# Sparse-head scores two units ahead, and three differential query projections moved up, in a one-core hybrid attention layer

## The chip, the cores and the metric

The kernel runs on one core of a Trainium2 chip. The metric is the device time of one execution in microseconds (us). TensorE is written PE, its weight loads PEld, VectorE DVE, ScalarE ACT, GpSimd POOL, and SyncE, which issues all DMAs here, SP.

## What is computed

One decoder layer over 1024 tokens of width 1024, batch 1, float32:

```python
h   = x @ w_in                                   # all queries, keys, values and gates
o_diff = diff_attention(dq, dk, dv, ...)         # 4 heads, two softmaxes each: p1 - lam * p2, then RMS norm
o_nsa  = nsa_attention(nq, ...)                  # 8 heads: compressed, selected and window branches, gated
mix = concat([o_diff, o_nsa]) @ w_out
x   = layer_norm(alpha * x + mix)
ffn = (silu(x @ w_gate) * (x @ w_up)) @ w_down   # d_ff = 2816
out = layer_norm(alpha * x + ffn)
```

With 16 selection blocks and top 16, the selected branch sees every causal key, so the kernel computes it as plain causal attention.

## The kernel before

All products of the projections and of the feed-forward part are done three times with float32 operands split in a high and a low half (`mm3`, lines 118 to 120). The keys and queries of attention carry both halves stacked in one 128-row operand, so a score block is two matmuls (lines 313 and 314). In the first 100 us x is loaded and the shared keys and values are made. From there to about 600 us attention runs, then the output projection, and from about 625 us the feed-forward part, whose matmuls stand in a fixed order.

Attention is a list of **units**. A unit of the sparse heads (`nsa_units`) is one pair of heads, one block of 128 queries and one kind, selected or window; eight blocks and two kinds make 16 units for each of four pairs p. A unit of a differential head (`diff_units`) is one head h and one block i. Each unit has two halves:

- the **front**: scores of both heads (or both softmax branches) into a PSUM bank `psS` (two of them in rotation), the addition of the position bias with a running minimum on DVE (line 320), which reads `psS` and writes a score tile `t`; exponentials on ACT (line 334); reciprocals on DVE and scaling on POOL;
- the **back**: transposes of the probabilities into `psT` (line 353 for the sparse heads, 343 for the differential ones), their copies to `pt` on ACT and DVE, and the products with the values into the one bank `psO` (lines 406, 414, 416, and 470).

There are six `t` tiles. A unit wider than 512 keys takes two of them, a narrower one takes one.

Beside the units stand **fillers**, projections that later units need: `qf` and `qdf` for one half (512 tokens) of the queries of a sparse pair or a differential head, `kf` and `kdf` for keys, `dvf` for values of a pair of differential heads. A filler of 512 tokens is 24 matmuls of 512 columns into a bank `psM` (two in rotation). A query half is evacuated by ACT (line 178) and DVE (line 179) and then spread by three DMAs on SP (line 163), of which the third overwrites what the first two read. Query halves live in two pairs of tiles in rotation, so a half can be evacuated only when the scores of the half two before it are done.

`phases` lists, phase by phase, the units, the fillers, and as its last number `look`: how many units may be pending, that is have their front issued and their back not. After each front, backs are issued until no more than `look` are pending. Fillers are handed out in list order in proportion to the backs that are done. Written order gives each instruction a priority (backs 60 lower, fillers 2000 lower than they stand); a scheduler then lays down one fixed order for each engine from priorities, dependences and free buffers. The engines keep that order at run time.

Of the kernel before, what the change touches and what calls it, by code (L numbers as in the profile page):

```python
# [39 lines left out]
def layer_kernel(ctx: ExitStack, tc: tile.TileContext, xT, x, w_t, w_vg, w_dv, lam_in, subln,  # L40
# [24 lines left out]
    def slot(n, dt=F32R, wide=False):  # L65

        w = 1024 + NC if n in (0, 6) else 1024
        t = slots.tile([P, w], dt, tag=f"slot{n}", name=f"slot{n}", bufs=1)
        return t if wide or w == 1024 else t[:, :1024]
# [35 lines left out]
    def w_tiles():  # L105
        lo = w_tile()
        return w_tile(), lo
# [38 lines left out]
    with ExitStack() as ctx_a:  # L146
# [363 lines left out]
        def k_fill(n, where, out, halves=(0, 1)):  # L510
            def steps():
                if 0 in halves:
                    out.extend([slot(m) for m in where])
                    out.append(load_split(w_t[n], *w_tiles(), l_eng="pool", pieces=2))
                for hf in halves:
                    yield from proj_steps(out[2], hf, evac_k(out))
            return steps, 5.2 * len(halves)
# [4 lines left out]
        def q_fill(n, hf, qt, tiles=w_tiles):  # L522

            def steps():
                if hf == 0:
                    qt.append(load_split(w_t[n], *tiles(), l_eng="pool", pieces=2))
                w = qt[0]

                def done(_, ps):
                    q = [q_tile() for _ in range(2)]  # L530
                    evac_q(q, qscale[:, n - 4:n - 3], ps)
                    qt.append(q)
                yield from proj_steps(w, hf, done)
            return steps, 5.2
# [3 lines left out]
        def dv_fill(pair, where, out, blocks, tiles):  # L538
            def steps():
                if pair not in dv_parts:  # L540
                    dv_parts[pair] = [(*load_split(w_dv[pair, :, kk, :], *tiles(kk), l_eng="pool", pieces=2), 4 * kk, 4)
                                      for kk in range(2)]
                parts = dv_parts[pair]
                for i in blocks:
                    if i % 4 == 0:
                        out.append(slot(where[i // 4], F32))
                    ps = ps_m()
                    yield from proj_rows(parts, 256, i, ps)
                    nc.scalar.copy(out[i // 4][:, (i % 4) * 256:(i % 4 + 1) * 256], ps[:, :256])
            return steps, 2.61 * len(blocks)  # L550
# [4 lines left out]
        def wo_copy(nh):  # L555
            def steps():
                for kp in range(KT // 2):
                    nc.sync.dma_start(wo_d[nh, kp], w_out[nh, kp])
                    yield 0.0
            return steps, 0.0  # L560
# [170 lines left out]
        def nsa(p):  # L731
            return lambda: nsa_units(p, qn[p], [KC[p // 2], K[p // 2][1]], [V[0][p // 2], V[1][p // 2]])
# [3 lines left out]
        def diff(h, first=0, last=NB):  # L736
            def f():
                if h not in made:
                    made[h] = diff_units(h, qd[h], kd[h], vd[h // 2])
                return made[h][first:last]  # L740
            return f

        def qf(p, hf):
            return q_fill(4 + p, hf, qn[p])

        def kf(hf):
            return k_fill(3, (), K[1], (hf,))

        def qdf(h, hf, tiles=w_tiles):
            return q_fill(8 + 2 * h, hf, qd[h], tiles)  # L750

        def kdf(h, hf):
            return k_fill(9 + 2 * h, ((0, 1), (2, 4))[h % 2], kd[h], (hf,))

        def dvf(pair, blocks):
            tiles = [lambda kk: w_tiles(), lambda kk: [slot(n) for n in ((10, 11), (3, 5))[kk]]][pair]
            return dv_fill(pair, ((8, 9), (6, 7))[pair], vd[pair], blocks, tiles)
# [7 lines left out]
        def held_fill():  # L765
# [8 lines left out]


        phases = [
            (nsa(0), [qf(0, 1), kf(0), qf(1, 0), kf(1)], 1, 0, 1),
            (nsa(1), [qf(1, 1), dvf(0, range(8)), wo_copy(0), qf(2, 0)], 1, 0, 1),
            (nsa(2), [qf(2, 1), kdf(0, 0), wo_copy(1), qf(3, 0), kdf(0, 1)], 1, 0, 1),
            (nsa(3), [qf(3, 1), kdf(1, 0), qdf(0, 0), kdf(1, 1)], 1, 0, 1),  # L780
            (diff(0), [qdf(0, 1), dvf(1, range(4)), qdf(1, 0)], 1, 0, 1),
            (diff(1), [qdf(1, 1), kdf(2, 0), kdf(2, 1), qdf(2, 0)], 1, 0, 1),
            (diff(2, 0, 4), [kdf(3, 0), kdf(3, 1), qdf(3, 0)], 0, 0, 2),
            (diff(3, 0, 4), [qdf(2, 1), dvf(1, range(4, 8))], 0, 0, 2),
            (diff(2, 4), [wo_fill(0), qdf(3, 1), wo_fill(1), held_fill(), out_fill(0, False), out_fill(1, False)], 0, 0, 2),
# [432 lines left out]
```

## Time and profile before

| | |
|---|---|
| median of 3 runs | 1329.98 us (1327.45 to 1330.0) |
| profiled execution | 1330.6 us, of which the span from the first to the last instruction is 1328.9 us |
| busy share of the span | PE 98%, PEld 83%, DVE 69%, ACT 49%, POOL 35% |
| mean granted TensorE clock | 0.997 |

The profiled execution is one of the kernel's ordinary executions; its own time is 0.6 us above the median. Busy time is the union of an engine's instructions. A matmul's record also covers the time in which its last columns drain, so two matmuls can start up to some 0.17 us later than they could have without any idle time showing between them.

### The profile page before, as it was taken

The numbers are of one execution on the slowest core, as the hardware profiler recorded it, in microseconds if no ns is written. First come the engines' busy times: TensorE is split into PE (matmuls) and PEld (weight loads), VectorE is DVE, ScalarE is ACT, GpSimd is POOL, SyncE is SP. The second block draws the span as 40 slices with busy tenths as digits, with TensorE's granted clock in tenths as the row PEclk, the third lists the DMA queues.
The fourth block names the chain that finished last, engine by engine and source line by source line (L and its number), as shares of the span: only waits on it lengthen the run. The fifth ranks groups of instructions, "written<-read, shape, count | busy, mean of one in ns | idle before, by whom it ended". The sixth has DMA issues, their size and how long they took to land.

```text
span 1328.9 us, 20438 instructions
## 1 busy us (share of the span) xinstructions
PE 1301.0 (98%) x6922; PEld 1106.2 (83%) x6922; DVE 914.9 (69%) x1949; ACT 649.1 (49%) x1398; POOL 469.7 (35%) x504
## 2 busy tenths in 40 slices
PE   9999999999999999999999999999999999999997
PEld 7898998888889878788887888788888888888886
DVE  5536658678798466684688758777777768555588
ACT  5336678676787455653345332332333326533330
POOL 4414354354445336553532222222312232000072
PEclk9999999999999999999999999999999999999999
DMA  9412022130211325533213656655455549768651
GB/s 356 137 26 63 7 59 50 31 80 19 62 24 45 72 60 156 174 102 113 103 72 96 220 191 222 204 169 190 158 191 188 190 147 350 270 202 285 191 171 66
DMA packets 86842, 183.13 MB, mean 138 GB/s; under 512 B 10577, under 2 KB 19153, under 8 KB 86609
## 3 DMA queue, kind: packets, MB, share of 16 engines
q1 hardware_dynamic: 86736, 181.82, 42.4%
q8 instruction: 55, 0.90, 0.3%
q14 instruction: 51, 0.41, 0.1%
HBM read 116.18 MB, written 57.15 MB: 130 GB/s over the span
## 4 chain that ended last, share of the span: by engine, by line
PE 86%; DVE 6%; DMA 3%; ACT 2%; issue 2%; POOL 0%; POOLq 0%; DVEq 0%; SPq 0%; ACTq 0%
PE psM L118 10%; PE psM L120 10%; PE psM L119 10%; PE psS L120 5%; PE psS L119 5%; PE psS L118 5%; PE psT L118 5%; PE psT L120 5%; PE psT L119 5%; PE psT L353 4%; PE psS L313 3%; PE psS L314 3%; PE psO L470 2%; PE psO L416 2%; PE psO L414 2%
## 5 line engine op out<-in xcount | busy, mean ns | idle before, releaser
L334 ACT ACTIVATE t<-t,m 128x128 f32<-128x128 f32 (+7 forms) x192 | 144.0, 750 | 67.9 <-DVE m L320 64.4
L399 POOL TENSOR_SCALAR t<-t,r,gates 128x640 f32<-128x640 f32 (+7 forms) x128 | 99.6, 784 | 188.7 <-DVE r L393 103.3
L313 PE MATMUL psS<-slot,q 128*128 128x320 f32 (+10 forms) x304 | 113.7, 377 | 8.9 <-DVE m L320 5.8
L118 PE MATMUL psM<-big,w 128*128 128x512 f32 x304 | 121.9, 401 | 0.3
L119 PE MATMUL psM<-big,w 128*128 128x512 f32 x304 | 120.1, 395 | 0.7 <-POOL big L85 0.7
L120 PE MATMUL psM<-big,w 128*128 128x512 f32 x304 | 119.8, 394 | 0.0
L976 POOL TENSOR_TENSOR half<-half,half 128x512 f32<-128x512 f32 x22 | 33.1, 1506 | 200.3 <-ACT half L975 200.3
L85 DVE TENSOR_TENSOR pt<-psT,pt 128x512 fp32r<-128x512 f32 (+1 forms) x152 | 91.2, 613 | 12.3 <-ACT pt L83 11.8
L314 PE MATMUL psS<-slot,q 128*128 128x320 f32 (+10 forms) x304 | 99.3, 329 | 0.0
L83 ACT CAST pt<-psT 128x512 fp32r<-128x512 f32 (+1 forms) x152 | 77.0, 526 | 31.5 <-PE psT L353 23.0
L83 ACT CAST big<-slot 128x1024 fp32r<-128x1024 f32 (+1 forms) x54 | 54.1, 1017 | 74.5 <-DVE slot L968 60.8
L353 PE MATMUL psT<-ident,t 128*128 128x128 f32 x528 | 84.0, 273 | 1.4 <-DVE pt L85 0.9
L85 DVE TENSOR_TENSOR op<-op 128x1024 fp32r<-128x1024 f32 x44 | 60.5, 1382 | 35.5 <-ACT op L83 34.9
L85 DVE TENSOR_TENSOR big<-slot,big 128x1024 fp32r<-128x1024 f32 (+1 forms) x54 | 63.5, 1182 | 29.7 <-ACT big L83 29.7
L313 PEld LDWEIGHTS psS<-slot,q 128*128 128x128 f32 x304 | 57.4, 189 | 24.2 <-DVE m L320 14.1
L83 ACT CAST op<-op 128x1024 fp32r<-128x1024 f32 x44 | 45.8, 1051 | 59.3 <-DMA op<-t_d 52.1
L320 DVE CUSTOM_DVE_ANT_0 t<-psS,dsel 128x384 f32<-128x384 f32 (+9 forms) x128 | 62.5, 493 | 16.5 <-PE psS L314 15.5
L980 POOL TENSOR_TENSOR half<-half,half 128x512 f32<-128x512 f32 x22 | 36.5, 1658 | 105.3 <-DVE half L979 97.8
L416 PE MATMUL psO<-pt,slot 128*128 128x256 f32 x264 | 72.8, 298 | 0.2
L414 PE MATMUL psO<-pt,slot 128*128 128x256 f32 x264 | 71.0, 288 | 0.1
L83 ACT CAST big<-big 128x1024 fp32r<-128x1024 f32 (+1 forms) x49 | 44.3, 913 | 48.8 <-DMA big<-t_d 39.0
L353 PEld LDWEIGHTS psT<-ident,t 128*128 128x128 f32 x528 | 61.7, 140 | 7.4 <-issue 3.2
(368 smaller groups left out, 3961.1 us busy)
## 6 DMA issues: line engine op xcount, KB each, us to landing
a_d<-slot SPq DMA_DIRECT2D x77, 256.0 KB, 3.0
t_d<-slot SPq DMA_DIRECT2D x77, 256.0 KB, 2.2
q<-q SPq DMA_DIRECT2D x48, 256.0 KB, 2.9
slot<-in_w_up_dram SPq DMA_DIRECT2D x22, 512.0 KB, 3.8
slot<-in_w_down_dram SPq DMA_DIRECT2D x22, 512.0 KB, 3.8
op<-a_d SPq DMA_DIRECT2D x44, 256.0 KB, 3.6
op<-t_d SPq DMA_DIRECT2D x44, 256.0 KB, 4.1
big<-a_d SPq DMA_DIRECT2D x33, 256.0 KB, 3.0
```

Of the source, the lines that this page charges most:

```text
L83: nc.scalar.copy(hi, src)
L85: eng.tensor_sub(lo, src, hi.bitcast(F32))
L118: nc.tensor.matmul(acc, lhsT=ah, rhs=bh, start=first, stop=False, skip_group_check=more)
L119: nc.tensor.matmul(acc, lhsT=ah, rhs=bl, start=False, stop=False, skip_group_check=more)
L120: nc.tensor.matmul(acc, lhsT=al, rhs=bh, start=False, stop=last, skip_group_check=more)
L313: nc.tensor.matmul(ps[:, :c + part], lhsT=q[0], rhs=k[:, ks], start=True, stop=False)
L314: nc.tensor.matmul(ps[:, :c + part], lhsT=q[1], rhs=k[:, ks], start=False, stop=True)
L334: nc.scalar.activation(t[:, :width], t[:, :width], AF.Exp, bias=m, scale=-1.0, accum_out=r)
L353: nc.tensor.transpose(tp[:rows, n * P:(n + 1) * P], s, ident)
L399: nc.gpsimd.tensor_scalar(t, t, r[:, c:c + 1], gates[:, i, gc:gc + 1], op0=ALU.mult, op1=ALU.mult)
L414: nc.tensor.matmul(po[:, :256], lhsT=v, rhs=pt[:, 0, n * 256:(n + 1) * 256], start=False, stop=False)
L416: nc.tensor.matmul(po[:, :256], lhsT=v, rhs=pt[:, 1, n * 256:(n + 1) * 256], start=False, stop=last)
```

## The change

`look` of the four sparse phases goes from 1 to 2, and in the phases of differential heads 0 and 1 a query projection moves ahead of other fillers. Nothing else is edited; every instruction is the same and only the order differs.

```diff
-            (nsa(0), [qf(0, 1), kf(0), qf(1, 0), kf(1)], 1, 0, 1),
-            (nsa(1), [qf(1, 1), dvf(0, range(8)), wo_copy(0), qf(2, 0)], 1, 0, 1),
-            (nsa(2), [qf(2, 1), kdf(0, 0), wo_copy(1), qf(3, 0), kdf(0, 1)], 1, 0, 1),
-            (nsa(3), [qf(3, 1), kdf(1, 0), qdf(0, 0), kdf(1, 1)], 1, 0, 1),
-            (diff(0), [qdf(0, 1), dvf(1, range(4)), qdf(1, 0)], 1, 0, 1),
-            (diff(1), [qdf(1, 1), kdf(2, 0), kdf(2, 1), qdf(2, 0)], 1, 0, 1),
+            (nsa(0), [qf(0, 1), kf(0), qf(1, 0), kf(1)], 1, 0, 2),
+            (nsa(1), [qf(1, 1), dvf(0, range(8)), wo_copy(0), qf(2, 0)], 1, 0, 2),
+            (nsa(2), [qf(2, 1), kdf(0, 0), wo_copy(1), qf(3, 0), kdf(0, 1)], 1, 0, 2),
+            (nsa(3), [qf(3, 1), kdf(1, 0), qdf(0, 0), kdf(1, 1)], 1, 0, 2),
+            (diff(0), [qdf(0, 1), qdf(1, 0), dvf(1, range(4))], 1, 0, 1),
+            (diff(1), [qdf(1, 1), kdf(2, 0), qdf(2, 0), kdf(2, 1)], 1, 0, 1),
             (diff(2, 0, 4), [kdf(3, 0), kdf(3, 1), qdf(3, 0)], 0, 0, 2),
             (diff(3, 0, 4), [qdf(2, 1), dvf(1, range(4, 8))], 0, 0, 2),
```

The first place is on PE, where differential head 1 passes from its block 6 (scores of 448 columns) to its block 7 (512 columns). `psS` takes scores, `psT` transposes, `psO` products with values, `psM` fillers. Before:

```order
L313 MATMUL psS<-slot_4550,q 128x448
L314 MATMUL psS<-slot_4550,q 128x448
L313 MATMUL psS<-slot_4550,q 128x448
L314 MATMUL psS<-slot_4550,q 128x448
L313 MATMUL psS<-slot_4549,q 128x512
L314 MATMUL psS<-slot_4549,q 128x512
L313 MATMUL psS<-slot_4549,q 128x512
L314 MATMUL psS<-slot_4549,q 128x512
L313 MATMUL psS<-slot_4550,q 128x512
L314 MATMUL psS<-slot_4550,q 128x512
L488 MATMUL psT<-ident,od 128x128 x4
```

The same four pairs of 512 columns in the changed kernel:

```order
L120 MATMUL psM<-big,w 128x512
L470 MATMUL psO<-slot_2216,pt 128x128 x4
L470 MATMUL psO<-slot_2558,pt 128x128
L313 MATMUL psS<-slot_4565,q 128x512
L488 MATMUL psT<-ident,od 128x128 x4
L314 MATMUL psS<-slot_4565,q 128x512
L313 MATMUL psS<-slot_4565,q 128x512
L314 MATMUL psS<-slot_4565,q 128x512
L343 MATMUL psT<-ident,t 128x128 x6
L313 MATMUL psS<-slot_4566,q 128x512
L314 MATMUL psS<-slot_4566,q 128x512
L343 MATMUL psT<-ident,t 128x128 x4
```

Five pairs that stood back to back are taken apart: fillers and products with values now stand between block 6 and block 7, and transposes between the pairs of block 7.

The second place is on SP, where the queries of differential head 3 (first half) are spread by their three DMAs (`q<-q`), beside loads of the output weights (`wo_d`) and of two rows of x (`in_x_dram`). Before:

```order
L101 DMA big<-wo_d 128x512 x8
L163 DMA q<-q 64x1024 x2
L574 DMA slot_7128<-in_x_dram 128x1024
L574 DMA slot_7239<-in_x_dram 128x1024
L163 DMA q<-q 64x1024
```

In the changed kernel:

```order
L101 DMA big<-wo_d 128x512 x8
L163 DMA q<-q 64x1024 x3
L574 DMA slot_7128<-in_x_dram 128x1024
L574 DMA slot_7239<-in_x_dram 128x1024
```

The third of the moves no longer stands behind the two loads of x.

The third place is on PE, in sparse pair 2, where the selected unit of block 7 (wide scores cut in pieces of 480 and 320 columns) meets the window unit. Before:

```order
L353 MATMUL psT<-ident,t 128x128 x4
L313 MATMUL psS<-slot_547,q 128x480
L314 MATMUL psS<-slot_547,q 128x480
L313 MATMUL psS<-slot_547,q 128x480
L314 MATMUL psS<-slot_547,q 128x480
L313 MATMUL psS<-slot_547,q 128x480
L314 MATMUL psS<-slot_547,q 128x480
L353 MATMUL psT<-ident,t 128x128 x4
L313 MATMUL psS<-slot_548,q 128x320
```

In the changed kernel:

```order
L313 MATMUL psS<-slot_547,q 128x480
L314 MATMUL psS<-slot_547,q 128x480
L353 MATMUL psT<-ident,pc 64x128
L353 MATMUL psT<-ident,t 128x128 x2
L313 MATMUL psS<-slot_547,q 128x480
L314 MATMUL psS<-slot_547,q 128x480
L353 MATMUL psT<-ident,t 128x128 x6
L353 MATMUL psT<-ident,pc 64x128
L313 MATMUL psS<-slot_547,q 128x480
L314 MATMUL psS<-slot_547,q 128x480
L313 MATMUL psS<-slot_548,q 128x320
L314 MATMUL psS<-slot_548,q 128x320
```

Transposes of an earlier unit now stand between the pieces of one unit's scores.

## Rows read from the trace of the kernel before

**Rows 1.** The page's first part: busy us (share of the span) and number of instructions, and from its fifth part the group of line 320 with its mean ns.

```profile
span 1328.9 us, 20438 instructions
PE 1301.0 (98%) x6922; PEld 1106.2 (83%) x6922; DVE 914.9 (69%) x1949; ACT 649.1 (49%) x1398; POOL 469.7 (35%) x504
...
L320 DVE CUSTOM_DVE_ANT_0 t<-psS,dsel 128x384 f32<-128x384 f32 (+9 forms) x128 | 62.5, 493 | 16.5 <-PE psS L314 15.5
```

**Rows 2.** Busy time of each engine in chosen stretches; the line ahead names the columns. The sparse phases lie in 100 to 425, the differential ones in 425 to 575.

```profile
core 0: us, PE busy (x) PEld busy (x) DVE busy (x) ACT busy (x) POOL busy (x), PEclk, DMA share, GB/s
100.00:425.00 325.00, 319.09 (x2151) 282.98 (x2150) 246.09 (x874) 242.02 (x660) 154.20 (x216) 1.00 0.19 45
350.00:375.00 25.00, 24.46 (x162) 20.32 (x161) 23.40 (x90) 22.85 (x68) 14.16 (x21) 1.00 0.28 65
425.00:575.00 150.00, 140.74 (x835) 120.92 (x834) 88.17 (x264) 85.53 (x226) 71.15 (x73) 0.99 0.40 112
550.00:575.00 25.00, 21.45 (x118) 16.02 (x118) 19.82 (x58) 19.26 (x48) 18.63 (x17) 1.00 0.47 136
725.00:750.00 25.00, 25.00 (x112) 20.71 (x111) 17.47 (x22) 7.24 (x12) 10.58 (x7) 1.00 0.61 212
```

**Rows 3.** Waits of PE and of its weight loads in 100 to 425: who waited for whom, us in total, times, longest.

```profile
PEld psS L313 <- DVE m L320: 7.7, 21, 0.7
...
PEld psS L313 <- PE psT L353: 1.8, 6, 0.6
...
PE psS L313 <- DVE m L320: 3.4, 11, 0.7
```

**Rows 4.** The same waits in 425 to 575.

```profile
PEld psS L313 <- DVE m L320: 6.4, 11, 1.1
PEld psS L313 <- DMA q<-q: 2.6, 1, 2.6
...
PE psO L470 <- ACT pt L346: 1.2, 1, 1.2
```

**Rows 5.** PE in order of time where head 1 passes from block 6 to block 7: start, us of the record, line, what it does, and in brackets the idle time before it and who ended it.

```profile
488.51 0.36 PE L314 MATMUL psS<-slot,q 128*128 128x448 f32 x1
488.71 0.37 PE L313 MATMUL psS<-slot,q 128*128 128x448 f32 x1
...
490.50 0.37 PE L314 MATMUL psS<-slot,q 128*128 128x448 f32 x1
491.63 0.47 PE L313 MATMUL psS<-slot,q 128*128 128x448 f32 x1 [0.77 <-DVE m L320]
491.94 0.37 PE L314 MATMUL psS<-slot,q 128*128 128x448 f32 x1
493.01 0.51 PE L313 MATMUL psS<-slot,q 128*128 128x512 f32 x1 [0.69 <-DVE m L320]
493.35 0.39 PE L314 MATMUL psS<-slot,q 128*128 128x512 f32 x1
493.84 0.50 PE L313 MATMUL psS<-slot,q 128*128 128x512 f32 x1
494.18 0.40 PE L314 MATMUL psS<-slot,q 128*128 128x512 f32 x1
494.64 0.50 PE L313 MATMUL psS<-slot,q 128*128 128x512 f32 x1
494.98 0.39 PE L314 MATMUL psS<-slot,q 128*128 128x512 f32 x1
495.82 0.63 PE L488 MATMUL psT<-ident,od 128*128 128x128 f32 x4 [0.46 <-DVE od L485]
...
497.47 0.28 PE L314 MATMUL psS<-slot,q 128*128 128x128 f32 x1
498.98 1.16 PE L470 MATMUL psO<-slot,pt 128*128 128x128 f32 x8 [1.24 <-ACT pt L346]
```

**Rows 6.** The way of head 3's first query half: the last matmul of its projection on PE, its evacuation on ACT (178) and DVE (179), its moves on SP, and the scores that wait for them; ahead of these the three moves of another half, with little other traffic. On SP the second number is the time from the first issue to the last issue's end.

```profile
474.00 4.72 SPq L163 DMA_DIRECT2D q<-q  x3
...
511.04 0.40 PE L120 MATMUL psM<-big,w 128*128 128x512 f32 x1
...
514.64 0.70 ACT L178 ACTIVATE q<-psM,qscale 128x512 fp32r<-128x512 f32 x1
...
515.89 0.74 DVE L179 SCALAR_TENSOR_TENSOR q<-psM,qscale,q 128x512 fp32r<-128x512 f32 x1
...
516.66 1.11 SPq L163 DMA_DIRECT2D q<-q  x2
517.87 1.87 SPq L574 DMA_DIRECT2D slot<-in_x_dram  x2
521.03 0.47 SPq L163 DMA_DIRECT2D q<-q  x1
...
526.23 0.33 PE L313 MATMUL psS<-slot,q 128*128 128x128 f32 x1 [2.39 <-DMA q<-q]
```

**Rows 7.** Granted clock behind that wait, by stretch (columns as in rows 2), and from the page's sixth part DMA issues with KB each and median us to landing.

```profile
526.00:528.00 2.00, 1.77 (x11) 1.77 (x12) 0.53 (x4) 0.90 (x5) 0.00 (x0) 0.73 0.79 161
528.00:530.00 2.00, 2.00 (x11) 2.00 (x10) 0.69 (x3) 1.34 (x4) 0.73 (x2) 0.50 0.01 4
...
q<-q SPq DMA_DIRECT2D x48, 256.0 KB, 2.9
```

## The prediction

> **What bounds the kernel now.** I read the page first: PE is busy 98% of the span and no other engine over 83% [rows 1], so only time in which PE waits can be won, 27.9 us of idle by that count. Then the stretches: in the feed-forward part 25 us hold 112 matmuls of 512 columns without idle time, 0.223 us each [rows 2]. That part is work alone and keeps its order, so the end moves by just as much as attention does. The idle time lies in the sparse phases (325 less 319.09, 5.9 us) and in the differential ones (150 less 140.74, 9.3 us) [rows 2].
>
> Idle time is too small a count. Of a score pair the first weight load and matmul wait until DVE has read the bank of two pairs ago. In the sparse phases the weight loads of scores waited 7.7 us for that in 21 cases, the matmuls 3.4 us by idle time [rows 3]; in the differential phases the loads waited 6.4 us in 11 cases [rows 4]. The rest is hidden under the records of matmuls that still drain. The Trainium skill's page "Perfetto Trace Analysis", section "Identifying the Most-Contended Engine", says that the busy share of matmuls is no good measure of how near TensorE is to its limit, since instructions overlap; the trace agrees, and by the busy share alone no more than 15.2 us would be there in attention.
>
> The wait chain is plain in the worst place. Between the third 448-wide pair of head 1's block 6 and the products behind block 7 [rows 5] the spacing of starts tells what is lost. An unhindered matmul of 448 columns is followed after 0.20 us (488.51 to 488.71), one of 512 after 0.223. Here follow 1.13, 1.07, 0.49, 0.46, 0.84 and, behind a 128-wide one (0.11), 1.51 us. Less the normal spacing these are 0.93, 0.87, 0.27, 0.24, 0.62 and 1.40, in all 4.3 us. DVE needs 0.49 us for a mean piece of scores [rows 1], PE puts out a pair in 0.4 to 0.45, and only two banks lie between them: pairs back to back run at DVE's pace.
>
> **What the change does, and its price.** No instruction is added or removed. Durations below are those of the profiled execution (1330.6 us, 0.6 above the median), and the sum is made against that.
>
> *Spacing of scores.* I walked both orders of PE with the spacings of the trace (0.223 us for 512 columns, less in proportion, 0.11 for a transpose) and counted, for each pair, the PE work between it and the pair that had its bank before. Before, 34 of 304 pairs have less than 0.8 us there, about as many as the 32 waits of loads [rows 3, 4]. In the changed order there are 22: 17 instead of 24 in the sparse phases, 5 instead of 10 in the differential ones.
>
> *Sparse phases, first term.* Seven fewer short pairs at 7.7/21 = 0.37 us would give 2.6 us; by visible idle alone 7 x 3.4/21 = 1.1, by the longest wait 7 x 0.7 = 4.9. But DVE is itself near its limit where most of the short pairs stand: 23.40 of 25 us in 350 to 375 [rows 2]. There one wait that goes leaves the next one longer. The order bears that out: in the second halves of pairs 1 and 3 the scores stand nearly as before, without fillers between them; the third place shown, in pair 2, is one of the better ones. I take 1.5 us, nearer to the visible idle, and keep 0 to 4.9. The priced cover is the same as before: exponentials, reciprocals and POOL's scaling stand behind more PE work, not less.
>
> *Differential head 1, second term.* The first half of head 1's queries is projected in the changed order while sparse pair 3 still runs, not behind all of head 0. The values of heads 2 and 3 then fill the passage from head 0 to head 1, and other fillers last into blocks 5 and 6 of head 1. So the five pairs shown back to back are apart, with transposes or fillers of 0.9 us and more between a pair and the next user of its bank, and the products that waited 1.40 us for their copy [rows 4, 5] stand further behind their transposes. Of the 4.3 us I leave 1.3 for the short pairs of head 2's first blocks that follow, and take 3.0. Bounds: 4.3 and 0.
>
> *Head 3's queries, third term.* Their scores waited 2.39 us [rows 6], the loads 2.6 [rows 4]. That wait has a second price: behind it the granted clock stood at 0.73 and 0.50 in the next two stretches of 2 us [rows 7], that is partly and then wholly at 1.2 in place of 2.4 GHz, where it had been at 2.4 before PE stood still; 2 x 0.27 + 2 x 0.50 makes 1.5 us. A shorter idle time, 1.24 us at 498.98, is followed by matmuls at full pace. Now what moves: in the changed order less filler work stands ahead of these scores, 9.8 us from the end of the projection (511.04 + 0.23 = 511.27) in place of 12.4, so PE comes to them at about 521.1. In return the third move stands ahead of two loads of x. Before, the moves took from 516.66 to 526.2, 9.5 us, with 5.2 for the third alone; another half shows 474.00 to 478.72, less 0.47 for the last issue, and then the median 2.9 to landing, 7.15 us in all [rows 6, 7]. The Trainium skill's page "DMA: Bandwidth & Descriptors", section "Queues, rings and completion order", says that each DMA engine takes a queue's descriptors in ring order; the 5.2 us of a third move behind two loads of 512 KB agree. On ACT line 178 also stands one exponential of 512 columns earlier, worth about what line 178 itself takes, 0.70 us [rows 6], and behind copies, so I take 0.5. The queries land at 516.1 + 7.15 = 523.3 and the wait is 2.2 us, hardly shorter. Whether the clock falls again is open between 1.24 and 2.39. I take 1.0 us of gain for the term (0.2 of wait and about half of the clock's 1.5). Bounds: 3.9 gained when the wait and the fall go, 2.7 lost when the moves take 9.5 us once more (526.2 less 521.1, less 2.4).
>
> What is queued behind: SP now waits for the first two moves with the x loads behind it, some 1.5 us later than before. These rows of x are first needed when the output projection adds them, after the second halves of heads 2 and 3 have begun, so nothing waits. The weight loads move with their fillers and stay ahead of them on SP.
>
> *Sum:* 1.5 + 3.0 + 1.0 = 5.5 us. 1330.6 less 5.5 is 1325.1.
>
> **The rivals.** A change of less than 0.2%, 2.7 us, is what a measurement of this kernel can't tell from none.
>
> *No change to speak of.* The waits only move. For it: DVE's 23.40 of 25 us [rows 2], and the fillers that now stand earlier are missing later: by head 3's first scores 2.6 us fewer matmuls of fillers lie ahead, and fewer lie between the scores of blocks 4 and 5 of head 2, just ahead of the stretch 550 to 575 that already loses 3.55 us of idle time [rows 2]. With the first and third term at 0 and 1.5 us of the second given back there, the time is 1330.6 - 1.5 = 1329.1. Against it: the count of short pairs falls in every part. Chance 0.22.
>
> *Slower.* With three sparse units in hand, the wide ones (i from 4 on, 4 pairs x 4 blocks x 2 kinds = 32 units) hold all six `t` tiles, so DVE can't read the next unit's scores until the transposes of the unit two before it are through, and PE behind it stands. The nearest row is the wait of score loads for transposes, 1.8 us in 6 cases, 0.3 each [rows 3]. At 0.3 in each of 32 units the cost is 9.6 us, and 1330.6 - 5.5 + 9.6 = 1334.7. It decides from 8.2/32 = 0.26 us a unit on, where the 5.5 are eaten and 2.7 lost besides. Against it: in the changed order of PE the transposes of the older unit still stand ahead of the wide scores, at nearly the same count of products done as before. Chance 0.12.
>
> *More than forecast.* The wait for head 3's queries goes with its clock (3.9) and the sparse phases give 2.6: with the 3.0 that is 9.5 us, 1321.1. Chance 0.12.
>
> **Numbers.** The forecast, 2.7 to 8 us faster, has 0.54: 1325.1. With the better case faster has 0.66, the same 0.22, slower 0.12. Its own range is 1322.6 to 1327.9. For 8 in 10 the range takes in the better case down to 1319.5, with 4.9 from the sparse phases on top of part of the rest, and reaches up to 1331.0, which holds the case of no change and leaves out the slower one and little else.
>
> **What the new profile would show.** First term: the loads of line 313 wait for line 320 in about 14 cases and 5 to 6 us in 100 to 425, not 21 and 7.7. Second: the passage from block 6 to 7 of head 1 without starts 1.1 us apart, the wait of line 470 for its copy gone, and fillers there. Third: one third move ahead of the x loads that lands within 3 us of its issue, a wait of about 2 us at head 3's first scores, and clock at 0.5 for some 3 us or not at all. The feed-forward part stays at 112 matmuls in 25 us. The forecast is wrong if DVE's waits on `t` tiles grow in the sparse phases, if idle time of 550 to 575 passes 5 us, or if the wait for `q` passes 4.

## The result and the profile after

The changed kernel takes 1315.95 us (median of 6, 1315.05 to 1317.69), the kernel before, timed beside it, 1328.08 (median of 6). The ratio is 0.9909, with a 95% interval of 0.9898 to 0.992: 12.1 us faster. The forecast was 1325.1, its range began at 1319.5. The direction was right and the size less than half of what came. The edit moves two query projections ahead of other fillers, `qdf(1, 0)` and `qdf(2, 0)`, not three as the title has it.

The page's first part, of the changed kernel (answers to [rows 1]; its profiled execution took 1317.69 us):

```profile
span 1316.0 us, 20436 instructions
PE 1293.5 (98%) x6922; PEld 1106.4 (84%) x6922; DVE 912.0 (69%) x1949; ACT 649.9 (49%) x1398; POOL 469.3 (36%) x504
```

Each engine does the same work, and PE's share is 98% again: by the page alone nothing happened. Busy time by stretch (answers to [rows 2]):

```profile
100.00:425.00 325.00, 319.76 (x2167) 287.37 (x2166) 246.77 (x874) 243.00 (x660) 153.36 (x215) 1.00 0.19 47
425.00:575.00 150.00, 144.52 (x884) 126.04 (x883) 95.15 (x289) 90.85 (x242) 77.05 (x78) 1.00 0.39 113
...
550.00:575.00 25.00, 22.60 (x136) 18.26 (x135) 18.81 (x59) 15.15 (x38) 12.13 (x12) 1.00 0.26 85
725.00:750.00 25.00, 25.00 (x112) 20.72 (x111) 17.43 (x25) 10.34 (x16) 3.79 (x2) 1.00 0.67 236
```

Between 425 and 575 us PE now does 884 matmuls where it did 835, and the feed-forward part still does 112 in 25 us: the gain lies in attention. Of the profiled spans' difference (1328.9 less 1316.0, 12.9 us) 1.8 us is no part of the change: behind 622 us the profiled execution of before took that much longer, and 1.5 to 2.3 us longer than any other kernel here. Most of it is one stall in the feed-forward part that stands in none of the others, 1.34 us from the start of the matmul ahead of it:

```profile
833.59 0.50 PE L118 MATMUL psO<-x21h,big 128*128 128x512 f32 x1 [0.95 <-ACT half L959]
```

The waits of PE and of its loads in 100 to 425 (answers to [rows 3]), then in 425 to 575 (answers to [rows 4]), changed kernel:

```profile
PEld psS L313 <- DVE m L320: 4.1, 11, 0.6
...
PEld psS L313 <- PE psT L353: 2.2, 8, 0.4
```

```profile
PEld psS L313 <- DVE m L320: 3.8, 6, 1.0
...
PEld psS L313 <- DMA q<-q: 1.2, 1, 1.2
```

The score loads' wait for DVE fell from 7.7 us in 21 cases to 4.1 in 11, and from 6.4 in 11 to 3.8 in 6. Their wait for transposes in the sparse phases grew a little, from 1.8 us [rows 3] to 2.2. The products of line 470 no longer wait for their copy. The passage into block 7 of head 1 (answers to [rows 5]):

```profile
487.53 0.39 PE L314 MATMUL psS<-slot,q 128*128 128x512 f32 x1
487.76 0.82 PE L343 MATMUL psT<-ident,t 128*128 128x128 f32 x6
488.33 0.47 PE L313 MATMUL psS<-slot,q 128*128 128x512 f32 x1
488.65 0.39 PE L314 MATMUL psS<-slot,q 128*128 128x512 f32 x1
488.88 0.60 PE L343 MATMUL psT<-ident,t 128*128 128x128 f32 x4
489.23 0.48 PE L313 MATMUL psS<-slot,q 128*128 128x512 f32 x1
489.55 0.39 PE L314 MATMUL psS<-slot,q 128*128 128x512 f32 x1
489.78 1.39 PE L470 MATMUL psO<-slot,pt 128*128 128x128 f32 x11
```

No brackets, so no idle time, and the spacings are those of the work: 0.23 us behind a matmul of 512 columns, 0.32 where its first one follows transposes. Before, they were 1.13 and 1.07 in such places. The way of head 3's first query half, and the stretch behind its scores' wait (answers to [rows 6, 7]):

```profile
504.95 0.71 ACT L178 ACTIVATE q<-psM,qscale 128x512 fp32r<-128x512 f32 x1
...
506.82 4.93 SPq L163 DMA_DIRECT2D q<-q  x3
511.85 1.22 SPq L574 DMA_DIRECT2D slot<-in_x_dram  x2
514.34 0.33 PE L313 MATMUL psS<-slot,q 128*128 128x128 f32 x1 [1.05 <-DMA q<-q]
```

```profile
516.00:518.00 2.00, 2.00 (x20) 2.00 (x18) 0.89 (x6) 0.77 (x3) 0.48 (x2) 1.00 1.06 347
```

The three moves stand together ahead of the loads of x, the wait is 1.05 us in place of 2.39, and the granted clock stays at 1.00, that is 2.4 GHz, behind it.

**Where the time went, by section.** Attention falls into sections that every kernel here runs in the same order, from the first scores of one sparse pair or differential head to those of the next. From a section's length I take off PE's work in it, each matmul with its unhindered spacing: 0.2265 us for 512 columns, the usual distance of starts in lines 118 to 120 (226 to 227 ns), less in proportion but at least 0.11, and 0.11 for a transpose. What is left is the time PE lost, the hidden part too. Sparse pair 2 of before, for one, runs from 246.5 to 335.7 us: 89.2 less 80.1 of work, 9.0 lost; in the changed kernel 81.9 less 75.9, 5.9 (a section's work differs since fillers move in and out). The table gives the loss before, and for every other kernel the difference to it, in us, from one profiled execution each. "Heads 2, 3 first" are their blocks 0 to 3, "second" the others with what follows up to 622 us of before, in the other kernels up to the same matmul. The first row hangs on the spacing: at 0.223 us, which the prediction got from 25 us and 112 records, of which some reach out of the stretch, it comes to 58.0 in all. The differences hardly do.

| | pairs 0, 1 | pair 2 | pair 3 | head 0 | head 1 | heads 2, 3 first | second | all |
|---|---|---|---|---|---|---|---|---|
| before, lost | 12.4 | 9.0 | 8.5 | 3.4 | 4.1 | 6.8 | 8.1 | 52.3 |
| changed kernel | -0.3 | -3.1 | -1.2 | +0.3 | -3.4 | -3.0 | -0.3 | -11.0 |
| look_only | -0.2 | -3.1 | -0.2 | +2.4 | 0 | -0.3 | -0.7 | -2.1 |
| fill_only | -0.1 | 0 | -0.1 | +0.6 | -3.4 | -3.2 | -2.5 | -8.7 |
| fill_d0 | 0 | 0 | 0 | +0.6 | -1.8 | -2.5 | -0.5 | -4.3 |
| fill_d1 | -0.1 | 0 | 0 | 0 | -2.7 | -3.0 | -0.1 | -5.9 |
| look_fill_d0 | -0.3 | -3.1 | -1.7 | +0.3 | -1.8 | -3.3 | -0.4 | -10.3 |
| look_fill_d1 | -0.3 | -3.1 | +0.9 | +2.5 | -2.7 | -3.1 | +0.2 | -5.7 |
| look_pair2 | -0.1 | -2.2 | +0.9 | 0 | 0 | -2.1 | -0.6 | -3.9 |
| look2_heads01 | -0.3 | -3.1 | -1.7 | +0.3 | -1.0 | -5.8 | -2.8 | -14.4 |
| look2_head1 | -0.3 | -3.1 | -1.7 | +0.3 | -3.5 | -3.6 | -2.8 | -14.6 |
| look_split4 | -1.2 | -3.0 | -0.2 | +1.8 | -0.2 | -3.0 | -3.2 | -9.1 |
| look_split_dve | -0.4 | -3.1 | -0.1 | +0.2 | -1.2 | -0.5 | -2.2 | -7.2 |
| after_split_dve | -0.4 | -3.1 | -1.5 | -0.5 | -0.4 | -0.3 | -2.2 | -8.5 |

The changed kernel's 11.0 us, the 1.8 behind 622 us and 0.3 ahead of the first scores make up the 12.9 between the profiles, to within 0.2.

The loss takes in the granted clock. It stood at 0.5 for 3.4 us at a time in heads 2, 3 first of before, `look_only`, `look_split4`, `look_split_dve` and `after_split_dve`, in the second halves of `fill_d1` and `look_fill_d1`, and in pair 3 of `look_fill_d1`. Half of 3.4, 1.7 us, is an estimate of what each costs.

### The profile page after: what moved, and what is told of

It is laid out like the page before. It is cut to its first block, busy times and chain, and to the rows that moved or that the text cites. A ratio compares the mean times of both kernels' runs of the same rounds, so it can differ in the third digit from the quotient of the medians.

```text
span 1316.0 us, 20436 instructions
## 1 busy us (share of the span) xinstructions
PE 1293.5 (98%) x6922; PEld 1106.4 (84%) x6922; DVE 912.0 (69%) x1949; ACT 649.9 (49%) x1398; POOL 469.3 (36%) x504
## 4 chain that ended last, share of the span: by engine, by line
PE 91%; DVE 4%; ACT 1%; DMA 1%; issue 1%; POOL 0%; POOLq 0%; SPq 0%; DVEq 0%; ACTq 0%
PE psM L118 11%; PE psM L120 10%; PE psM L119 10%; PE psT L118 6%; PE psT L119 6%; PE psT L120 6%; PE psS L120 6%; PE psS L118 6%; PE psS L119 6%; PE psT L353 4%; PE psS L313 3%; PE psS L314 3%; PE psO L416 2%; PE psO L414 2%; PE psO L470 2%; PE psO L119 2%
## 5 line engine op out<-in xcount | busy, mean ns | idle before, releaser
L118 PEld LDWEIGHTS psM<-big,w 128*128 128x128 f32 x304 | 57.3, 188 | 13.6 <-DVE q L179 1.7
```

Source lines behind the costliest of these rows:

```text
L118: nc.tensor.matmul(acc, lhsT=ah, rhs=bh, start=first, stop=False, skip_group_check=more)
```

## The experiments

**The two halves of the change apart.** First the sparse phases alone (`look_only`):

```diff
-            (nsa(0), [qf(0, 1), kf(0), qf(1, 0), kf(1)], 1, 0, 1),
+            (nsa(0), [qf(0, 1), kf(0), qf(1, 0), kf(1)], 1, 0, 2),
...
-            (nsa(3), [qf(3, 1), kdf(1, 0), qdf(0, 0), kdf(1, 1)], 1, 0, 1),
+            (nsa(3), [qf(3, 1), kdf(1, 0), qdf(0, 0), kdf(1, 1)], 1, 0, 2),
```

> Only the sparse phases' look goes from 1 to 2; the fillers stay as before. The theory that the parts add: the sparse phases lost 4.2 us less in the changed kernel (score loads waited 4.1 in place of 7.7 us for DVE), so this kernel is 4 to 5 us faster than before, ratio about 0.9965, and everything from head 0 on is as before: the wait for head 3's queries of about 2.4 us and the half clock behind it are still there. The rival that the fillers alone did it (the gain in the sparse phases comes from the query projection that moved into pair 3): within 1 us of before, ratio 0.999 to 1.001.

Measured 1326.51 us against 1328.13, ratio 0.9991 (0.9981 to 1.0): next to nothing, but not for the rival's reason. Pair 2 gains its 3.1 us without any filler move, and head 0 gives 2.4 back. Then the two filler moves alone (`fill_only`):

```diff
-            (diff(0), [qdf(0, 1), dvf(1, range(4)), qdf(1, 0)], 1, 0, 1),
-            (diff(1), [qdf(1, 1), kdf(2, 0), kdf(2, 1), qdf(2, 0)], 1, 0, 1),
+            (diff(0), [qdf(0, 1), qdf(1, 0), dvf(1, range(4))], 1, 0, 1),
+            (diff(1), [qdf(1, 1), kdf(2, 0), qdf(2, 0), kdf(2, 1)], 1, 0, 1),
```

> Both query projections moved up, look stays 1. Parts add: 7 to 8 us faster, ratio about 0.9943, with the passage inside head 1 clean, a wait of about 1 us for head 3's queries and no half clock. Fillers alone: 12 us faster, ratio 0.991, and the waits of score loads in the sparse phases near 4 us in place of 7.7.

Measured 1320.63, ratio 0.995 (0.9935 to 0.9965), 7.5 us. The halves gain 1.6 and 7.5, together 9.1 and not 12.1: by these medians 3 us come only when both are there.

**Each filler move alone.** The first (`fill_d0`), then the second (`fill_d1`):

```diff
-            (diff(0), [qdf(0, 1), dvf(1, range(4)), qdf(1, 0)], 1, 0, 1),
+            (diff(0), [qdf(0, 1), qdf(1, 0), dvf(1, range(4))], 1, 0, 1),
```

> Only the projection of head 1's first query half moves ahead of the values of heads 2 and 3. My prediction gave this move the passage in head 1 (3.0 us). By the order of PE the four short bank distances there stay (0.5 us), so now I expect little of it: 1 us faster (ratio 0.9993) from sparse pair 3, where three short pairs go, and the wait for head 3's queries with its half clock as before. If the prediction's reading holds, 3 us or more (ratio 0.9977).

```diff
-            (diff(1), [qdf(1, 1), kdf(2, 0), kdf(2, 1), qdf(2, 0)], 1, 0, 1),
+            (diff(1), [qdf(1, 1), kdf(2, 0), qdf(2, 0), kdf(2, 1)], 1, 0, 1),
```

> Only the projection of head 2's first query half moves ahead of its second key half. By the order this move alone takes the short bank distances out of head 1's blocks 6 and 7 (0.5 to 1.6 and more) and puts the third query move of head 3 ahead of the x loads on SP. Expected: 5 to 6 us faster, ratio 0.9957: 3 from the passage, 1.2 of the wait for head 3's queries and 1.7 of the half clock. If the passage needs both moves: about 3 us, ratio 0.9977.

Measured 1324.15, ratio 0.9974 (0.9965 to 0.9984), and 1322.82, ratio 0.9962 (0.9948 to 0.9976): 4.0 and 5.3 us. I had expected 1 us of the first, or 3 and more if the prediction reads it rightly. In head 1 the first move gives back 1.8 us, the second 2.7 and both 3.4, so they reach partly for the same stall. So it is with head 3's queries: 2.5, 3.0 and 3.2 us in "heads 2, 3 first". The last line of [rows 4] is the wait of line 470 for its copy, 1.2 us. The same wait in the kernel with the first move alone:

```profile
PE psO L470 <- ACT pt L346: 1.3, 1, 1.3
```

It stays there, and it is gone in every kernel with the second move. The waits of the scores for DVE, 1.5 us of idle time in 440 to 500 before, fall to 0.2 with either.

The largest of these, 0.77 us at 491.63 [rows 5], was not DVE's pace alone. DVE and POOL just ahead of it in the kernel before:

```profile
489.57 1.33 DVE L452 SCALAR_TENSOR_TENSOR r<-r,lam,r 128x1 f32<-128x1 f32 x1
489.61 1.28 POOL L85 TENSOR_TENSOR w<-w 128x512 fp32r<-128x512 f32 x1 [8.88 <-ACT w L83]
...
490.90 0.67 DVE L320 CUSTOM_DVE_ANT_0 t<-psS,dsel,m 128x448 f32<-128x448 f32 x1
```

An operation on one column, 0.22 us long elsewhere, ended with POOL's subtraction, and the read of the bank (line 320) stood behind it. In `look_only` and `look_pair2`, whose head 1 runs as before, the 1.33 us and the wait are there again; in `fill_d0`, `fill_d1` and the changed kernel line 452 takes 0.22 us at most in this place. How much of the gain in head 1 is this, and how much the spacing of the pairs, no run tells apart.

**What the look alone costs in head 0.** In the kernel with the look alone PE stands in head 0 at 417.51; PE, then DVE, then POOL around it:

```profile
417.51 0.55 PE L343 MATMUL psT<-ident,t 128*128 128x128 f32 x3 [0.92 <-DVE t L454]
```

```profile
414.40 1.17 DVE L482 TENSOR_SCALAR r<-r 128x4 f32<-128x4 f32 x1
415.48 1.31 DVE L452 SCALAR_TENSOR_TENSOR r<-r,lam,r 128x1 f32<-128x1 f32 x1
416.82 0.64 DVE L454 SCALAR_TENSOR_TENSOR t<-t,r 128x400 f32<-128x400 f32 x1
...
414.26 2.50 POOL L85 TENSOR_TENSOR w<-w 128x512 fp32r<-128x512 f32 x2
```

Two operations on four columns and one column take 1.17 and 1.31 us, and each ends just as one of POOL's two subtractions ends. I then took the look with each filler move (`look_fill_d0`, `look_fill_d1`):

```diff
             (nsa(3), ..., 1, 0, 2),
-            (diff(0), [qdf(0, 1), dvf(1, range(4)), qdf(1, 0)], 1, 0, 1),
+            (diff(0), [qdf(0, 1), qdf(1, 0), dvf(1, range(4))], 1, 0, 1),
```

> Look 2 in the sparse phases and, of the two filler moves, only that of head 1's first query half. With look alone the trace shows sparse pair 2 at 3.1 us less loss but head 0 at 2.5 us more; with both changes head 0 has only 0.2 more. Theory: the filler move in diff(0) is what takes away that loss in head 0 (its projection then runs in sparse pair 3 and the fillers of head 0 start later), so this kernel is 8.5 to 9.5 us faster than before (ratio 0.993 to 0.9936). Rival: the loss in head 0 belongs to look and only the move in diff(1) hides it: 5 to 6 us faster (ratio 0.9957).

```diff
             (nsa(3), ..., 1, 0, 2),
-            (diff(1), [qdf(1, 1), kdf(2, 0), kdf(2, 1), qdf(2, 0)], 1, 0, 1),
+            (diff(1), [qdf(1, 1), kdf(2, 0), qdf(2, 0), kdf(2, 1)], 1, 0, 1),
```

> The sparse look of 2 and only the second query move (head 1's phase). Theory: the parts of the change add up except where the first query move (head 0's phase) takes away what the look alone costs in head 0. So here, without that move, they add up: 1326.51 + 1322.82 - 1328.13 = 1321.2 us (1320.4 to 1322.0), with the wait of 0.9 us of transposes (L343) for DVE's L454 near 417.5 us still there, as in the run with the look alone. Rival: any query move that comes earlier does it, and the parts gain more than their sum whichever one it is: 1318 to 1319.5 us, wait gone.

Measured 1319.66, ratio 0.9943 (0.9927 to 0.9959), 8.9 us; and 1321.95 against 1327.66, ratio 0.9958 (0.9944 to 0.9972), 5.7 us. With the first move head 0's loss is gone (+0.3 for +2.4) and pair 3 gains besides (-1.7). With the second it stays at +2.5, with the same wait as above (0.9 us, L343 for L454), and the time lies in the theory's range: 5.7 us against 1.6 and 5.3, no gain by being together. So the look and the first move gain together what they don't alone: 8.9 us against 1.6 and 4.0 by time, 10.3 against 2.1 and 4.3 in the table. For the whole change the table has no such surplus (11.0 against 2.1 and 8.7): what head 0 and pair 3 gain, the second halves take back, which gain 2.5 us in `fill_only` and 0.3 here. So the 3 us by which the timed medians pass the sum of the parts are not placed in full.

**POOL's part in it.** The splitting of the value weights in four pieces (`look_split4`), then on DVE (`look_split_dve`), each with the look alone:

```diff
-load_split(w_dv[pair, :, kk, :], *tiles(kk), l_eng="pool", pieces=2)
+load_split(w_dv[pair, :, kk, :], *tiles(kk), l_eng="pool", pieces=4)
```

> The look of 2 alone, and POOL's subtractions that split the value weights (L85) cut in four pieces of 256 columns instead of two of 512. Theory: an operation of DVE on 128x1 or 128x4 (L452, L482) that meets such a subtraction ends only with it, so it lasts up to 1.34 us now and at most 0.75 us here where it meets a value weight's piece (0.64 us each); PE's wait for L454 near 417.5 us falls from 0.92 to under 0.4 us, and head 0 gets about 1 us shorter. Rival: these operations are long for another reason (DVE's own queue), and stay at 1.0 to 1.3 us with the wait at about 0.9. The scheduler plans anew with the other pieces, so times may move elsewhere; the durations decide.

```diff
-load_split(w_dv[pair, :, kk, :], *tiles(kk), l_eng="pool", pieces=2)
+load_split(w_dv[pair, :, kk, :], *tiles(kk), l_eng="dve", pieces=2)
```

> The look of 2 alone, with the value weights split on DVE (128x512 each, 0.7 us of DVE) and none of those on POOL. Theory of the long small operations: L452 and L482 stay under 0.6 us in head 0, since POOL has no subtraction there, at the price of 4 x 0.7 us of DVE in the same place; the wait for L454 near 417.5 us gone. Rival: DVE is simply too busy in head 0 with two units in hand: then 2.8 us more work makes PE's waits for DVE in 405 to 425 longer than in the run with the look alone.

DVE's and POOL's rows with the four pieces:

```profile
411.73 0.69 DVE L452 SCALAR_TENSOR_TENSOR r<-r,lam,r 128x1 f32<-128x1 f32 x1
414.54 1.28 DVE L482 TENSOR_SCALAR r<-r 128x4 f32<-128x4 f32 x1
415.74 1.30 DVE L452 SCALAR_TENSOR_TENSOR r<-r,lam,r 128x1 f32<-128x1 f32 x1
...
410.28 2.82 POOL L85 TENSOR_TENSOR slot<-w,slot 128x256 fp32r<-128x256 f32 x4
...
414.51 2.51 POOL L85 TENSOR_TENSOR w<-w 128x512 fp32r<-128x512 f32 x2
```

The one that meets a 256-wide value piece lasts 0.69 us where it lasted 1.03. But the costly two meet subtractions that I had taken for the value weights and that are not: they are still 512 wide, so these two are as long as before, and PE stands 1.40 us behind them (its scores at 417.57). With the values split on DVE, POOL's order shifts, and nothing of it lies beside the two:

```profile
415.09 0.20 DVE L482 TENSOR_SCALAR r<-r 128x4 f32<-128x4 f32 x1
415.21 0.21 DVE L452 SCALAR_TENSOR_TENSOR r<-r,lam,r 128x1 f32<-128x1 f32 x1
```

Now they take 0.2 us, the wait is gone and head 0 loses +0.2 and not +2.4, although two of the value weights' subtractions, 1.3 us, now lie on DVE there: the rival (DVE is simply too busy) falls. That wait was 1.1 us of the 2.4 by its spacing; the rest is spread over smaller ones. Their total times, 1320.21 and 1321.12 in one execution each, differ from the look alone for other reasons too: with other pieces the scheduler lays down another order everywhere (the table's right half).

**The same in the changed kernel** (`after_split_dve`).

```diff
-load_split(w_dv[pair, :, kk, :], *tiles(kk), l_eng="pool", pieces=2)
+load_split(w_dv[pair, :, kk, :], *tiles(kk), l_eng="dve", pieces=2)
```

> The changed kernel with the value weights split on DVE in place of POOL. If long small operations of DVE beside POOL's subtractions still cost time in the changed kernel, it gains up to the 1 to 2 us of their excess: 1314 to 1315.5 us. If DVE's own work counts more there, it stays at 1316 or loses up to 2.8 us for eight subtractions that lie where DVE is nearly full: 1316 to 1318.8 us. I hold the second for likelier, since in head 0 of the changed kernel only one such operation (1.1 us) is left.

Measured 1323.47, ratio 0.9966 (0.9953 to 0.9979): 7.5 us slower than the changed kernel, far beyond both expectations. Its profiled execution (1320.04) says where part of it is: head 1 gains 0.4 and not 3.4, and head 3's queries come late again (2.75 us, with the clock at half behind it, as the rows below show). Where the other executions spend a further 3 to 4 us no profile shows.

**The look in pair 2 alone** (`look_pair2`).

```diff
-            (nsa(2), [qf(2, 1), kdf(0, 0), wo_copy(1), qf(3, 0), kdf(0, 1)], 1, 0, 1),
+            (nsa(2), [qf(2, 1), kdf(0, 0), wo_copy(1), qf(3, 0), kdf(0, 1)], 1, 0, 2),
```

> Look 2 in sparse pair 2 alone. Theory that a phase gains by its own look: pair 2 loses 3 us less than before, the other pairs nothing, as in the kernel with look 2 everywhere. Rival, by the order: pair 2's order changes little here (23 short pairs in all in place of 24, against 16 with look 2 everywhere), so what pair 2 gained came with the place at which pairs 0 and 1 hand over their fillers: less than 1 us.

Measured 1324.6 in one execution. Pair 2 gains 2.2 us by its own look, nearer to the theory than to the rival, and pair 3 gives 0.9 back. More telling is the clock behind head 3's queries. PE's wait for the moves in this kernel, and the stretch that follows; then both for the look alone; then the scores and the following stretch in `after_split_dve`:

```profile
PE psS L313 <- DMA q<-q: 1.9, 1, 1.9
```

```profile
524.00:526.00 2.00, 2.00 (x18) 2.00 (x19) 0.73 (x6) 1.15 (x6) 0.00 (x0) 1.00 0.70 150
```

```profile
PE psS L313 <- DMA q<-q: 2.0, 1, 2.0
```

```profile
524.00:526.00 2.00, 1.51 (x7) 1.51 (x8) 0.60 (x4) 0.40 (x2) 0.00 (x0) 0.63 0.92 188
526.00:528.00 2.00, 2.00 (x12) 2.00 (x11) 0.69 (x3) 1.95 (x8) 0.73 (x2) 0.51 0.04 10
```

```profile
518.88 0.33 PE L313 MATMUL psS<-slot,q 128*128 128x128 f32 x1 [2.75 <-DMA q<-q]
```

```profile
520.00:522.00 2.00, 2.00 (x11) 2.00 (x11) 0.87 (x5) 0.73 (x4) 0.56 (x2) 0.50 0.56 148
```

Behind 1.9 us of waiting the clock stayed at 2.4 GHz, behind 2.0 and 2.75 it went to 1.2. In the same place 0.7 to 1.3 us (fill_only, fill_d1, look_fill_d0, fill_d0, the changed kernel) left it alone as well.

**Deeper look in heads 0 and 1.** On top of the changed kernel, in both heads (`look2_heads01`), then in head 1 alone (`look2_head1`):

```diff
-            (diff(0), [qdf(0, 1), qdf(1, 0), dvf(1, range(4))], 1, 0, 1),
-            (diff(1), [qdf(1, 1), kdf(2, 0), qdf(2, 0), kdf(2, 1)], 1, 0, 1),
+            (diff(0), [qdf(0, 1), qdf(1, 0), dvf(1, range(4))], 1, 0, 2),
+            (diff(1), [qdf(1, 1), kdf(2, 0), qdf(2, 0), kdf(2, 1)], 1, 0, 2),
```

> The changed kernel with look 2 also in the phases of heads 0 and 1. By the order 21 short pairs in place of 22, and head 3's first scores stand 11.8 us of PE work behind the end of their projection in place of 9.8. Theory that waits read off the order decide: the wait for head 3's queries (1.05 us) goes, with it 1 to 2 us, ratio to before 0.989 to 0.990. Rival: no better than the changed kernel (0.9909), since the stretch behind loses what is won.

```diff
-            (diff(1), [qdf(1, 1), kdf(2, 0), qdf(2, 0), kdf(2, 1)], 1, 0, 1),
+            (diff(1), [qdf(1, 1), kdf(2, 0), qdf(2, 0), kdf(2, 1)], 1, 0, 2),
```

> The changed kernel with look 2 in the phase of head 1 alone: 21 short pairs, head 3's scores 11.1 us behind their projection. Theory as in the kernel before this one: ratio to before 0.9895 to 0.9905. Rival: as the changed kernel, 0.9909.

Measured 1314.32, ratio 0.9903 (0.9887 to 0.992), and 1314.6, ratio 0.9903 (0.9888 to 0.9917). Their spans in the profile are 1312.1 and 1311.8, about 4 us below the changed kernel's, but these executions are the fastest of four each and the changed kernel's was the slowest of six. The medians are 1.4 and 1.6 us lower and the ratios overlap with its own: a gain over the changed kernel is not shown. In `look2_heads01` the scores of head 3 do not wait for their queries any more.

## Why the prediction was wrong in size

**Where it counted from.** The sum was taken from 1330.6 us, the profiled execution of before, with the stall above in it. The median of the six beside the changed kernel is 1328.08, and none of the 42 other executions of before took more than 1330.0; so 2.5 of the 9.1 us by which 1325.1 was missed lie there. All three terms stayed inside their bounds; the range let only one or two of them be high at once.

**First term, sparse phases: forecast 1.5, measured 4.6** (0.3 + 3.1 + 1.2; the bounds were 0 and 4.9). The step that failed is the price: a count of short pairs at a mean wait, discounted. I took 1.5 for a count that gave 2.6, because DVE is busy 23.40 of 25 us in 350 to 375 [rows 2]. That stretch lies in pair 3, and there the look by itself gains 0.2, as the step says. But the gain is made in pair 2, 3.0 to 3.1 us in each of the nine kernels with the look in all four pairs. (Pair 3's other 1.0 comes with the first filler move, whose projection now runs there; by itself that move gains nothing in the pair.) One stretch had been made to speak for four phases.

The count would have misplaced it too. By pair it goes from 6, 6, 5 and 7 short pairs to 5, 5, 3 and 4, with the look alone to 5, 5, 3 and 3: two fewer give 0.3 us in pairs 0 and 1 together and 3.1 in pair 2, four fewer give 0.2 in pair 3. What falls is the sum of all waits of the weight loads in pair 2, from 7.4 us in 22 cases to 3.9 in 14; in pairs 0 and 1 it stays (2.2 and 5.1 us before, 2.2 and 5.0 in the changed kernel). Busy time of the four sections before the change:

```profile
84.00:175.00 91.00, 90.06 (x627) 83.23 (x626) 59.54 (x216) 58.81 (x163) 34.66 (x51) 1.00 0.14 34
175.00:246.50 71.50, 70.40 (x463) 61.38 (x461) 54.95 (x205) 56.25 (x157) 34.71 (x51) 1.00 0.21 53
246.50:335.70 89.20, 87.31 (x534) 74.41 (x533) 61.79 (x217) 60.74 (x165) 42.77 (x60) 1.00 0.22 51
335.70:399.60 63.90, 62.49 (x431) 54.59 (x429) 56.19 (x207) 55.45 (x155) 28.72 (x45) 1.00 0.16 39
```

DVE works 65, 77, 69 and 88% of pairs 0 to 3. Its load fits the difference of pairs 2 and 3, but not pair 0, which has as much room as pair 2 and gains hardly anything. Why the gain falls in pair 2 stays open. Of its load waits, the prediction had counted those for line 320 alone; those for transposes and copies fall as well. Load waits in pair 2 (246 to 336) before, then in the changed kernel (246 to 328):

```profile
PEld psS L313 <- DVE m L320: 2.1, 5, 0.7
PEld psS L313 <- PE psT L353: 1.2, 3, 0.6
...
PEld psO L416 <- DVE pt L85: 1.0, 4, 0.3
```

```profile
PEld psS L313 <- DVE m L320: 1.4, 4, 0.6
...
PEld psS L313 <- PE psT L353: 0.6, 2, 0.4
PEld psO L416 <- DVE pt L85: 0.5, 2, 0.3
```

These three lose 1.8 us, of which line 320 is only 0.7. (The third place of the change, 480 columns wide, is block 6 of pair 2; the pieces of block 7 are 320, 384 and 384 wide.) In all sparse phases the mark came short as well: 11 cases and 4.1 us, not 14 and 5 to 6.

**The look's own price, missed.** No rival held that the look costs 2.4 us in head 0. I said only that the exponentials, reciprocals and scaling behind it had enough cover. The first filler move takes that price away, so the forecast did not suffer for it.

**Second term, head 1: forecast 3.0, measured 3.4 in head 1,** right in place and nearly in size, with the marks that I named. The reason was half right. I put it all down to the first move; alone it gives 1.8 and leaves the 1.3 us wait for the copy, which the second takes away. And I read the stall as DVE's pace, 0.49 us a piece, where DVE was held beside POOL for 1.1 us just ahead of the first wait (1.33 for 0.22 us).

**Third term, head 3's queries: forecast 1.0, measured 3.0** (heads 2 and 3, first blocks). The moves went as forecast: all three ahead of the x loads, 506.82 to 514.30, 7.5 us (7.15 forecast). The wait was 1.05 and not 2.2, because PE came later than I had it: 8.3 us after the evacuation began on ACT (513.29 less 504.95), where I had reckoned 7.0 (521.1 less 514.1, half a microsecond ahead of 514.64). So the part of the term that failed is the chance given to the clock: its half, 0.75, became the whole 1.5. The order on SP is not needed for that. With the look and the first move the third move still stands behind the x loads:

```profile
509.31 1.87 SPq L574 DMA_DIRECT2D slot<-in_x_dram  x2
512.45 0.47 SPq L163 DMA_DIRECT2D q<-q  x1
```

There the moves take 9.3 us again (508.10 to 517.37), but PE comes later, the wait is 0.73 us and the section gains 3.3.

**Not in the sum: the second halves of heads 2 and 3.** The filler moves together gain 2.5 us there, and the changed kernel keeps 0.3 of it. I had looked there for losses alone (550 to 575 passing 5 us of idle; it has 2.4). Alone the moves gain 0.5 and 0.1, the second with a stretch at half clock in it, worth some 1.7 us; what makes the 2.5 is open.

**The rivals.** No change and slower are refuted: in the changed kernel's sparse phases DVE waits for transposes 0.2 us in one case, as before, and score loads wait for them 2.2 us in 8 cases, 0.4 more than before where the slower case needed 8.2. The better case, 9.5 us, named the right two places, pair spacing and the clock, and was still short.

## What to carry to other kernels

Price a change of order phase by phase, each with the load of the engine that sets the pace in that phase; one saturated stretch says nothing about the next phase, and a count of short distances in the order does not say in which phase they cost. Parts of a reordering don't add up, and any edit that moves the plan shifts waits of 1 to 3 us in places it doesn't name. A transfer whose wait is near 2 us is worth more than its wait, since the clock's fall behind it can cost 1.5 us again.

## What the hardware showed unexpectedly

Some operations of DVE wait for POOL. L452, on one column, takes 0.20 to 0.22 us alone, and 0.69 beside a 256-wide subtraction, up to 1.36 beside a 512-wide one (`look_fill_d1`), ending with it; L451, a reciprocal on the same column, takes 0.14 to 0.17 wherever it lies. A second operand is not what marks them: L482, which multiplies four columns by a constant, goes from 0.15 to 0.20 us to 1.17 in the rows above. Nor is it small size: L454 on 400 columns takes 0.62 to 0.66 us, and 1.54 in `look_only` at 554.96, behind a 512-wide subtraction begun 0.2 us ahead of it. The Trainium skill's page "SBUF — State Buffer", section "SBUF: two separate sides", says that VectorE and GpSimd share one pair of ports under an exclusive lock, which a VectorE operation takes in a two-port mode or with two operands in SBUF, and that the one that comes later is held up for the other's whole instruction; the trace agrees, in the rows of 414 and 415 us above. For which of the two reasons L482 is held no run here shows.

The clock fell behind a wait of 2.0 us and not behind one of 1.9. Idle time alone does not tell it: in the kernel with the second move alone it fell at 552.5, behind one idle time of 1.50 us in the records (PE for a subtraction of POOL, with starts 1.9 us apart), and in the changed kernel an idle time of 1.1 us for the same subtraction left it at 1.00. In `look_fill_d1` it fell at 358.0, 2 us behind an idle time of 1.29 us, where 1.31 us for head 3's queries in `fill_d0` left it. What else decides is open.
